# Decayed cumulative sum of a matrix product: the last five lumps of output on other queues

## The chip, the cores and the metric

The kernel runs on one core of one Trainium2 chip. The metric is the time of one execution in microseconds (us), the median of several runs; less is better. The core has a matrix engine (TensorE, PE in the profile), a vector engine (VectorE, DVE), an activation engine (ScalarE, ACT), a general engine (GpSimd, POOL) and an engine that here only issues transfers (SyncE, SP). Each engine carries out its own instructions in order. A transfer (DMA) is an instruction in the order of the engine that issues it; the data are then moved by 16 DMA engines that all queues share.

## The reference

```python
B, S, D = (16, 2048, 1024)
xw = x @ w
out[:, 0, :] = xw[:, 0, :]
for t in range(1, S):
    out[:, t, :] = decay[None, :] * out[:, t - 1, :] + xw[:, t, :]
```

All arrays are float32. `decay` holds 1024 values between 0.05 and 0.95. The output is 134 MB.

## The kernel before, in words

Time is cut into chunks of 512 steps, 64 in all (4 for each of the 16 batches), and most of the work takes two chunks of a batch together. The 1024 output columns are cut into 8 groups of 128. A **tile** is one group of columns for one pair of chunks: 128 partitions (columns) by 1024 steps. The last two chunks are taken singly, so the last 16 tiles have 512 steps. There are 31 x 8 + 16 = 264 tiles, and the text counts the last ones from the end: tile -1 is the last, tile -16 the first of the short ones.

For each tile TensorE multiplies eight blocks of w with x (converted to bf16 and transposed beforehand) into PSUM (`matmul`, L131). Then the recurrence runs along time, in one of two ways. An unpaired tile is scanned by VectorE straight from PSUM (`run`, L221). A paired tile has the scan over every second step only: ScalarE copies PSUM out (`copy`, L183, letter `p`) and multiplies the even steps by the decay (`odd`, `g`, through `decayed`, L169), GpSimd adds (`join`, L196, `j`), VectorE scans with the squared decay (`scan`, L201, `S`), and ScalarE (`even`, `h`) and GpSimd (`fill`, L246, `c`) compute the steps between. `z` sets the first value, `k` saves the last one for the next chunk. At last VectorE turns the tile back so that time lies on partitions (`back`, L258, `B`), writing it into an output buffer `ot`.

Four tiles, that is 512 columns, share one output buffer, which is written out as a whole: this is a **lump**, with the class `Outlet` to hold it. There are four such buffers, taken in turn, so a lump's first transpose must wait until the lump four before it has been stored. A lump of long tiles is 2 MB, a lump of short ones 1 MB. It is stored by four DMAs, one for each quarter of the partitions (`q`, 32 partitions each), in runs of 512 bytes. They are issued when the fourth tile has been transposed, in `store` (L282). Nearly all lumps are stored by SyncE alone, in the order of quarters 0, 2, 1, 3. Four lumps near the end (tiles -24 to -9) alternate between SyncE (quarters 0 and 1) and GpSimd (quarters 2 and 3); the next one (tiles -8 to -5) goes by SyncE alone in eight DMAs, each with half of the steps. The four last tiles are not transposed by VectorE: the function `ending` (L387 to L393) has TensorE transpose them, ScalarE and VectorE copy them out by turns, and SyncE store them in four DMAs of 256 KB.

The order of the work of ScalarE, VectorE, GpSimd and SyncE around each tile is written out by hand in the table `agenda`: a row for each step, with the deeds in their order, a letter and a tile. Everything issued is kept in that order on its engine (`pin`), and the semaphores between engines, among them the counters on which DMAs report that they are done, are set by the framework when it schedules the program. DMAs of SyncE and ScalarE use eight such counters, taken in turn; GpSimd's DMAs use eight others. A DMA waits until the DMA that had its counter before it has landed.

The rows of `agenda` for the last steps, before the change, with the transposes (`B`) of the lumps in question:

```python
-19: "p-20 g-20",
-18: "j-20 S-19 S-20 k-19 B-19",
-13: "p-14 S-16 g-14 j-14 S-15 h-16 k-16 c-16",
-9: "p-10 k-12 g-10 h-12 B-11 j-10 k-11",
-6: "p-7 g-7 j-7 B-10 B-8",
-3: "p-4 B-6 g-4 B-5 j-4",
-1: "S-2 h-4 c-4 a-1 b-1 V",
```

Of the kernel before, what the change touches and what calls it, by code (L numbers as in the profile page):

```python
# [14 lines left out]
def _ap(ap_obj: bass.AP, new_ap, extra_offset=0):  # L15
    return dataclasses.replace(
        ap_obj,
        ap=[list(p) for p in new_ap],
        offset=ap_obj.offset + extra_offset,
    )  # L20
# [5 lines left out]
def kernel(  # L26
# [26 lines left out]
    nc = tc.nc  # L53
    pin = tc.keep_in_program_order
    B, S, D = x.shape
# [3 lines left out]
    P = 32  # L59
# [6 lines left out]
    R = K // 2  # L66
    CH = D // 2
    CR = CH // NQ
# [7 lines left out]
    def ring(pool, name, count, shape, dtype=FP32):  # L76
        i = turns[name] = turns.get(name, -1) + 1
        return pool.tile(shape, dtype, name=f"{name}{i % count}")

    def quad(q):  # L80
        return slice(q * P, (q + 1) * P)
# [12 lines left out]
    def ot_tile(nj):  # L94
        return ring(sb, "ot", 4, [128, nj, CR])
# [29 lines left out]
    def matmul(ps, n, k, xt, t0=0, t1=TL, start=0, pairs=None):  # L125
        if pairs is None:
            rhs = xt[:, k // 2, k % 2, t0:t1]
        else:
            rhs = pairs[:, k // 2, t0 // P:t1 // P, :, k % 2].rearrange("p j i -> p (j i)")
        lhs = wsb[:, k, n].rearrange("p q i -> p (q i)")  # L130
        pin(nc.tensor.matmul(  # L131
            out=ps[:, t0:t1] if ps.shape[1] >= t1 else ps,
            lhsT=lhs,
            rhs=rhs,
            start=(k == 0 and t0 == start),
            stop=(k == K - 1),
        ))
# [3 lines left out]
    class Tile:  # L141
# [3 lines left out]
        def __init__(self, g, n, ps, outlets):  # L145
            self.b, self.t0 = chunks[g[0]]
            self.T = TL * len(g)
            self.n, self.ps, self.outlets = n, ps, outlets
            self.paired = n % R != R - 1
            if len(tiles) in flips or len(tiles) - len(slots) in flips:  # L150
                self.paired = not self.paired
            self.turn = len(tiles)
            self.lot = sum(t.paired for t in tiles)
            self.prev = None if self.t0 == 0 else last[n]
            if self.t0 + self.T < S:
                last[n] = const.tile([128, 1], FP32, name=f"keep{n}", bufs=2)
                self.keep = last[n]
            else:
                self.keep = None
# [106 lines left out]
    class Outlet:  # L266


        def __init__(self, ns, nj, half=0, queues=(nc.sync,), pieces=1):
            self.pieces = pieces  # L270
            self.ns, self.missing, self.half = ns, set(ns), half
            self.nj, self.t0, self.queues = nj, half * nj * P, queues
            self.ot = ot_tile(nj)

        def store(self, b, t0):
            n0 = self.ns[0]
            c0 = n0 % R * P
            size = len(self.ns) * P
            nj = self.nj // self.pieces
            for j in range(0, self.nj, nj):  # L280
                for i, q in enumerate((0, 2, 1, 3)):
                    pin(self.queues[i % len(self.queues)].dma_start(  # L282
                        out=_ap(out, [[D, P], [P * D, nj], [1, size]],
                                (b * S + t0 + self.t0 + j * P) * D
                                + n0 // R * CH + q * CR + c0),
                        in_=self.ot[quad(q), j:j + nj, c0:c0 + size]))

# [1 line left out]
    size = M * CH  # L291
# [37 lines left out]
    for q in range(NQ):  # L329
        pin(nc.sync.dma_start(  # L330
            out=rows[q * P:q * P + R],
            in_=_ap(decay, [[P, R], [CH, 2], [1, P]], q * CR)))
# [71 lines left out]
    slots = [(g, n) for g in groups[:-1] for n in range(K)]  # L404
    slots += [([c], n) for c in groups[-1] for n in range(K)]
    tiles = []

    def turn_and_load(c):
# [24 lines left out]
        "d": square_again,  # L433
        "I": identity,
        "V": ending,
        "p": lambda s: tiles[s % len(slots)].copy(),
        "g": lambda s: tiles[s % len(slots)].odd(),
        "z": lambda s: tiles[s % len(slots)].zero(),
# [42 lines left out]
        32: "c29 S31 S30 h30 B29 c30 p32 g32 z32 j32 B30 B31 L L",  # L481
        33: "p33 g33 z33 j33 S32 h32 c32 k32 L L",
        -20: "z-20",
        -19: "p-20 g-20",
        -18: "j-20 S-19 S-20 k-19 B-19",
        -17: "h-20 k-20 c-20 S-18 k-18",
        -16: "I S-17 B-20 p-16 g-16 j-16",
        -15: "z-15 k-17 B-18 z-16",
        -14: "p-15 g-15 z-14 j-15 B-17",
        -13: "p-14 S-16 g-14 j-14 S-15 h-16 k-16 c-16",  # L490
        -12: "S-13 h-15 k-15 c-15 S-14 k-13",
        -11: "p-12 B-13 h-14 B-15 g-12 c-14 k-14 B-16",
        -10: "j-12 B-14 z-12 S-12 z-10 S-11",
        -9: "p-10 k-12 g-10 h-12 B-11 j-10 k-11",
        -8: "S-9 c-12 S-10 k-9",
        -7: "z-7 B-12 h-10 k-10 B-9 c-10 S-8",
        -6: "p-7 g-7 j-7 B-10 B-8",
        -5: "S-7 S-6 h-7 c-7",
        -4: "z-4 S-5 B-7",
        -3: "p-4 B-6 g-4 B-5 j-4",  # L500
        -2: "S-3 S-4",
        -1: "S-2 h-4 c-4 a-1 b-1 V",
    }
# [24 lines left out]
    def rest(s):  # L528
        do = [f"S{s - 1}"] if tiles[s - 1].paired else []
        do.append(f"C{s - 1}")  # L530
        if tiles[s - 2].paired:
            do.append(f"B{s - 2}")
        return do + [f"B{s - 1}"] + later.get(s, []) + ["L"] * len(loads)
# [7 lines left out]
    for step, (g, n) in enumerate(slots):  # L541
        T = TL * len(g)
        left = step - len(slots)
        if n % R == 0:
            ns, nj = range(n, n + R), T // P
            both = -6 * R <= left < -2 * R
            outlets = [Outlet(ns, nj, queues=(nc.sync, nc.gpsimd) if both else (nc.sync,),
                              pieces=2 if left == -2 * R else 1)]
        if left == -R:
            outlets = []  # L550
        if step == 0:
            heads = [ring(psp, "ps", 3, [128, T]) for _ in range(3)]
            firsts = [ps[:, 0:TL] for ps in heads] + [spares[0]]
            seconds = [ps[:, TL:T] for ps in heads] + [spares[1]]
            for j0, j1 in halves:
                for k in range(0, K, 2):
                    for i in range(R):
                        matmul(firsts[i], i, k, xt_of[0], j0 * P, j1 * P, pairs=xw_of[0])
            for k in range(1, K, 2):
                for i in range(R):  # L560
                    matmul(firsts[i], i, k, xt_of[0])
            for k0 in range(0, K, 2):
                for i in range(R):
                    for k in (k0, k0 + 1):
                        matmul(seconds[i], i, k, xt_of[1], 0, H * P,
                               pairs=xw_of[1] if k0 < 4 else None)
            for i in range(R):
                for k in range(K):
                    matmul(seconds[i], i, k, xt_of[1], H * P, TL, H * P,
                           pairs=xw_of[1] if i < 2 else None)  # L570
        if step < R:
            ps = heads[n] if n < 3 else tuple(spares)
        else:
            if step == K + 1:
                ps = nexts
            elif len(g) == 2 or n % R < 3:
                ps = ring(psp, "ps", 3, [128, T])
            else:
                ps = ring(psp, "spare", 1, [128, TL])
            todo = [(k, l) for k in range(K) for l in range(len(g))]  # L580
            if step < K:
                todo.sort(key=lambda kl: kl[0] % 2)
            elif step == K:
                todo = []
                nexts = ring(psp, "ps", 3, [128, T])
                for l in range(len(g)):
                    for i, both in enumerate((ps, nexts)):
                        for k in range(K):
                            matmul(both[:, l * TL:(l + 1) * TL], n + i, k, xt_of.get(g[l]),
                                   pairs=xw_of[g[l]] if g[l] in (3,) else None)  # L590
            elif step == K + 1:
                todo = []
            if left == -1:
                ps = tuple(both[:, t:t + TL // 2] for t, both in zip(
                    (0, TL // 2), (ps, ring(psp, "ps", 3, [128, TL]))))
                for t, half in zip((0, TL // 2), ps):
                    for k in range(K):
                        matmul(half, n, k, xt_of[g[0]], t, t + TL // 2, t)
                todo = []
            for k, l in todo:  # L600
                matmul(ps[:, l * TL:(l + 1) * TL], n, k, xt_of[g[l]])
        tiles.append(Tile(g, n, ps, outlets))
        do = agenda.get(step, agenda.get(left) if left >= -20 else None)
        if do is None:
            do = usual(step)
        else:
            do = do.split()
            if left == -20:
                do = rest(step) + do
        perform(do)  # L610
# [29 lines left out]
```

## Time and profile before

| | us |
|---|---|
| median of 3 runs | 908.35 (907.34 to 908.75) |
| span of the profiled execution | 907.2 |
| PE busy | 892.8 (98%) |
| DVE busy | 826.3 (91%) |
| ACT busy | 686.2 (76%) |
| POOL busy | 663.0 (73%) |
| POOL, issues of output stores (L282), 8 of them | 5.7 busy, 5.5 idle before them |
| DMA, mean over the span | 226 GB/s |

No time is recorded for the profiled execution itself beside its span; the span is 1.2 us below the median of the runs. The span is that of the instructions on the core's engines, the waits for the last transfers among them. "Busy" is the time in which an engine has an instruction under way; issues of DMAs by SyncE and ScalarE are not counted. A line of the profile gives the source line, the engine, the operation, what it writes and reads, its count, the busy time and the mean of one, and then the idle time before it with the work whose end ended most of it. SPq and ACTq are the queues in which SyncE and ScalarE issue transfers; an issue is over when its descriptors are handed on, and "to landing" is the time from the start of the issue until the data are reported stored.

### The profile page before, as it was taken

The page shows a single profiled execution, that of the slowest core. Times are in us where ns is not written, and L with a number is a line of the kernel's source. Part 1 is how long each engine was busy: PE and PEld are TensorE (multiplying, and loading weights), DVE is VectorE, ACT ScalarE, POOL GpSimd, SP SyncE. Part 2 cuts the span into 40 slices and gives each one's busy share as a digit, 9 for nine tenths or more (in the row PEclk, how much of TensorE's full clock was granted, in tenths as well). Part 3 has the DMA queues.
Part 4 walks back from the last instruction along what each step waited for, and adds up shares of the span by engine and source line. Part 5 has one row for each costly group of instructions (what it writes and reads, how often), then busy time and mean ns, then how long its engine had stood idle before and what let it go on. Part 6 is the DMA issues. An engine that isn't in the chain of part 4 may idle for free.

```text
span 907.2 us, 12004 instructions
## 1 busy us (share of the span) xinstructions
PE 892.8 (98%) x4119; PEld 411.4 (45%) x4201; DVE 826.3 (91%) x628; ACT 686.2 (76%) x955; POOL 663.0 (73%) x763
## 2 busy tenths in 40 slices
PE   9999999999999999999999999999999999999996
PEld 5444444444444444444444444444444444444443
DVE  4999989999999999899999999999999999999996
ACT  4889867777777877877877778778778778777742
POOL 7888678877777767768677777777677686776562
PEclk9999999999999999999999999999999999999999
DMA  9999999999999999999999999999999999999788
GB/s 194 194 215 220 227 215 220 215 238 255 249 250 254 241 243 259 247 244 228 227 233 227 227 232 227 226 232 233 220 230 231 228 231 223 232 229 207 153 161 211
DMA packets 397230, 204.77 MB, mean 226 GB/s; under 512 B 8816, under 2 KB 395376, under 8 KB 397168
## 3 DMA queue, kind: packets, MB, share of 16 engines
q1 hardware_dynamic: 258960, 131.62, 59.6%
q0 software_dynamic: 137920, 71.85, 58.1%
q8 instruction: 33, 0.54, 0.2%
q10 hardware_dynamic: 288, 0.52, 0.2%
q14 instruction: 29, 0.24, 0.1%
HBM read 138.42 MB, written 134.22 MB: 301 GB/s over the span
## 4 chain that ended last, share of the span: by engine, by line
PE 93%; DMA 2%; POOL 1%; issue 1%; DVE 1%; ACT 0%; POOLq 0%; DVEq 0%
PE ps L131 93%; DMA xb<-in_x_dram 2%; POOL ot L299 1%; POOL xb L105 1%; PE spare L131 1%; DVE xw L115 0%; ACT xt L123 0%; ACT xs L183 0%; DVE so L201 0%; PE spare L387 0%; DVE ot L258 0%; ACT h L169 0%; PE ps L387 0%; POOLq L635 0%; POOL xs L196 0%
## 5 line engine op out<-in xcount | busy, mean ns | idle before, releaser
L131 PE MATMUL ps<-xt,wsb 128*128 128x512 bf16 x3942 | 863.5, 378 | 4.7 <-ACT h L169 0.2
L131 PEld LDWEIGHTS <-wsb 128*128 128x128 bf16 x4152 | 405.9, 98 | 479.9 <-ACT wsb L306 0.8
L196 POOL TENSOR_TENSOR xs<-h,xs 128x512 f32<-128x512 f32 (+1 forms) x190 | 243.0, 1279 | 181.8 <-ACT h L169 79.4
L183 ACT COPY xs<-ps 128x1024 f32<-128x1024 f32 (+1 forms) x190 | 189.4, 997 | 155.3 <-PE ps L131 144.2
L258 DVE STREAM_TRANSPOSE ot<-so 128x1024 f32<-128x1024 f32 (+1 forms) x260 | 300.1, 1191 | 2.1 <-POOL so L190 1.1
L246 POOL TENSOR_TENSOR so<-h,xs 128x512 f32<-128x512 f32 (+1 forms) x190 | 241.4, 1272 | 39.0 <-ACT h L169 25.7
L123 ACT COPY xt<-xw 128x2048 bf16<-128x2048 bf16 (+1 forms) x136 | 242.3, 1790 | 7.8 <-DVE xw L115 7.6
L105 POOL DMA_DIRECT2D xb<-in_x_dram x264 | 174.3, 661 | 3.3 <-DMA ot<-in_w_dram 1.1
L169 ACT ACTIVATE h<-so,dec 128x512 f32<-128x512 f32 (+1 forms) x190 | 145.4, 766 | 27.7 <-DVE so L201 24.4
L115 DVE STREAM_TRANSPOSE xw<-xb 128x2048 f32<-128x2048 f32 (+1 forms) x78 | 147.4, 1901 | 5.5 <-DMA xb<-in_x_dram 5.5
L201 DVE TENSOR_TENSOR_SCAN so<-spare,keep,xs 128x512 f32<-128x512 f32 (+1 forms) x97 | 120.0, 1239 | 27.7 <-POOL xs L196 27.4
L201 DVE TENSOR_TENSOR_SCAN so<-spare,xs 128x512 f32<-128x512 f32 x93 | 113.3, 1220 | 27.6 <-POOL xs L196 24.6
L169 ACT ACTIVATE h<-ps,dec 128x512 f32<-128x512 f32 (+1 forms) x190 | 130.3, 686 | 0.0
L221 DVE TENSOR_TENSOR_SCAN so<-dec,ps 128x1024 f32<-128x1024 f32 x34 | 76.8, 2261 | 1.0 <-ACT h L169 1.0
L221 DVE TENSOR_TENSOR_SCAN so<-dec,keep,ps 128x1024 f32<-128x1024 f32 (+1 forms) x35 | 75.9, 2169 | 0.1
L250 ACT COPY keep<-so 128x1 f32<-128x1 f32 x136 | 25.3, 189 | 9.9 <-DVE so L221 9.4
L192 ACT COPY so<-keep 128x1 f32<-128x1 f32 x97 | 18.4, 191 | 2.6 <-DVE ot L258 2.4
L131 PE MATMUL ps<-xw,wsb 128*128 128x256 bf16 (+1 forms) x68 | 11.2, 301 | 0.1
L190 POOL MEMSET so<- 128x1 f32 x93 | 10.7, 117 | 0.6 <-DVE ot L258 0.6
L131 PE MATMUL spare<-xt,wsb 128*128 128x512 bf16 (+1 forms) x48 | 10.0, 335 | 0.0
L282 POOL DMA_DIRECT2D out_dram<-ot x8 | 5.7, 722 | 5.5 <-DVE ot L258 5.1
L299 POOL DMA_DIRECT2D ot<-in_w_dram x12 | 6.6, 546 | 3.3 <-DMA xb<-in_x_dram 2.0
(38 smaller groups left out, 44.5 us busy)
## 6 DMA issues: line engine op xcount, KB each, us to landing
out_dram<-ot SPq DMA_DIRECT2D x244, 512.0 KB, 10.9
xb<-in_x_dram POOLq DMA_DIRECT2D x248, 256.0 KB, 7.8
xb<-in_x_dram POOLq DMA_DIRECT2D x16, 128.0 KB, 5.8
out_dram<-ot POOLq DMA_DIRECT2D x4, 512.0 KB, 11.6
ot<-in_w_dram POOLq DMA_DIRECT2D x12, 128.0 KB, 5.1
out_dram<-ot SPq DMA_DIRECT2D x4, 256.0 KB
out_dram<-ot POOLq DMA_DIRECT2D x4, 256.0 KB, 8.5
out_dram<-ot SPq DMA_DIRECT2D x8, 128.0 KB, 4.3
```

The costliest lines, as they stand in the source:

```text
L105: pin(nc.gpsimd.dma_start(out=xb_of[c][quad(q), j0:j1], in_=_ap(x, [[D, P], [P * D, j1 - j0], [1, CQ]], (b * S + t0 + j0 * P) * D + q * CQ)))
L115: pin(nc.vector.transpose(out=dst.rearrange("p (m j i) -> p j m i", m=M, i=P)[:, j0:j1, m0:m1], in_=src.rearrange("p (j m c) -> p j m c", ...
L123: pin(copy(out=xt_of[c][:, m0:m1, :, j0 * P:j1 * P], in_=src))
L131: pin(nc.tensor.matmul(out=ps[:, t0:t1] if ps.shape[1] >= t1 else ps, lhsT=lhs, rhs=rhs, start=(k == 0 and t0 == start), stop=(k == K - 1),))
L169: pin(nc.scalar.activation(out=h, in_=src, func=mybir.ActivationFunctionType.Copy, scale=dec[:, self.n:self.n + 1]))
L183: pin(nc.scalar.copy(out=self.xs, in_=self.ps))
L196: pin(nc.gpsimd.tensor_tensor(out=odds, in0=self.g, in1=odds, op=ALU.add))
L201: pin(nc.vector.tensor_tensor_scan(out=so[:, 3:T + 2:2], data0=squares[-1][:, n:n + 1].to_broadcast([128, T // 2]), data1=self.xs[:, 1:T:2 ...
L221: pin(nc.vector.tensor_tensor_scan(out=so[:, t + 2:t + 2 + size], data0=dec[:, n:n + 1].to_broadcast([128, size]), data1=ps, initial=befor ...
L246: pin(nc.gpsimd.tensor_tensor(out=self.so[:, 2:T + 2:2], in0=self.h, in1=self.xs[:, 0:T:2], op=ALU.add))
L250: pin(nc.scalar.copy(out=self.keep, in_=self.so[:, self.T + 1:self.T + 2]))
L258: pin(nc.vector.transpose(out=outlet.ot[:, :, c0:c0 + P], in_=self.so[:, 2 + t0:2 + t0 + nj * P].rearrange("p (i t) -> p i t", t=P)))
```

## The change

The four lumps that went half by SyncE and half by GpSimd, and the fifth that went by SyncE in eight pieces, now all go half by SyncE (quarters 0 and 1, issued as before when the lump is complete) and half by ScalarE (quarters 2 and 3). ScalarE's half has a deed of its own, `O`, with a place of its own in the table: `O-21` stands for the lump whose last tile is -21. `O-21` comes after `g-20`, `O-17` after `g-14`, `O-13` before `p-10`, `O-9` after `g-7` and `O-5` after `g-4`. The pieces are gone. Nothing else in the table is moved.

```diff
-        def __init__(self, ns, nj, half=0, queues=(nc.sync,), pieces=1):
-            self.pieces = pieces
+        def __init__(self, ns, nj, half=0, shared=False):
             self.ns, self.missing, self.half = ns, set(ns), half
-            self.nj, self.t0, self.queues = nj, half * nj * P, queues
+            self.nj, self.t0, self.shared = nj, half * nj * P, shared
             self.ot = ot_tile(nj)
 
         def store(self, b, t0):
+            self.b, self.at = b, t0 + self.t0
+            self.send(nc.sync, (0, 1) if self.shared else (0, 2, 1, 3))
+
+        def send(self, queue, quads):
             n0 = self.ns[0]
             c0 = n0 % R * P
             size = len(self.ns) * P
-            nj = self.nj // self.pieces
-            for j in range(0, self.nj, nj):
-                for i, q in enumerate((0, 2, 1, 3)):
-                    pin(self.queues[i % len(self.queues)].dma_start(
-                        out=_ap(out, [[D, P], [P * D, nj], [1, size]],
-                                (b * S + t0 + self.t0 + j * P) * D
-                                + n0 // R * CH + q * CR + c0),
-                        in_=self.ot[quad(q), j:j + nj, c0:c0 + size]))
+            for q in quads:
+                pin(queue.dma_start(
+                    out=_ap(out, [[D, P], [P * D, self.nj], [1, size]],
+                            (self.b * S + self.at) * D + n0 // R * CH + q * CR + c0),
+                    in_=self.ot[quad(q), :, c0:c0 + size]))
...
+        "O": lambda s: tiles[s % len(slots)].outlets[0].send(nc.scalar, (2, 3)),
...
-        -19: "p-20 g-20",
+        -19: "p-20 g-20 O-21",
...
-        -13: "p-14 S-16 g-14 j-14 S-15 h-16 k-16 c-16",
+        -13: "p-14 S-16 g-14 O-17 j-14 S-15 h-16 k-16 c-16",
...
-        -9: "p-10 k-12 g-10 h-12 B-11 j-10 k-11",
+        -9: "O-13 p-10 k-12 g-10 h-12 B-11 j-10 k-11",
...
-        -6: "p-7 g-7 j-7 B-10 B-8",
+        -6: "p-7 g-7 j-7 B-10 O-9 B-8",
...
-        -3: "p-4 B-6 g-4 B-5 j-4",
+        -3: "p-4 B-6 g-4 B-5 j-4 O-5",
...
-            both = -6 * R <= left < -2 * R
-            outlets = [Outlet(ns, nj, queues=(nc.sync, nc.gpsimd) if both else (nc.sync,),
-                              pieces=2 if left == -2 * R else 1)]
+            outlets = [Outlet(ns, nj, shared=left >= -6 * R)]
```

On each engine the rest of the instructions keeps its order. GpSimd loses its eight stores, ScalarE gains ten, and SyncE has two stores instead of eight for lump -5.

## The prediction

> Six lumps of output matter, named by their last tile counted from the end of the 264: -25 (2 MB, by SyncE alone in both kernels), -21 and -17 (2 MB), -13, -9 and -5 (1 MB). Times are us from the start of the profiled span.
>
> **What bounds the kernel now.** First the page's parts 2 and 4:
>
> ```profile
> PE   9999999999999999999999999999999999999996
> PE 93%; DMA 2%; POOL 1%; issue 1%; DVE 1%; ACT 0%; POOLq 0%; DVEq 0%
> ```
>
> TensorE sets the pace until the last tiles; a change to stores can only act in the tail. The chain's last piece there is `DVE h L391`, the last copy of the ending, which ends at 899.73; the span ends at 907.16. VectorE and SyncE's queue in the tail (start, length, engine, line, operation, count):
>
> ```profile
> 882.86 0.71 DVE L258 STREAM_TRANSPOSE ot<-so 128x512 f32<-128x512 f32 x1
> ...
> 887.66 1.27 DVE L258 STREAM_TRANSPOSE ot<-so 128x512 f32<-128x512 f32 x2
> ...
> 899.04 0.69 DVE L391 COPY h<-spare 128x512 f32<-128x512 f32 x1 [0.18 <-PE spare L387]
> ```
>
> ```profile
> 893.73 6.97 SPq L282 DMA_DIRECT2D out_dram<-ot  x8
> 900.80 1.45 SPq L393 DMA_DIRECT2D out_dram<-xb  x3
> 902.66 0.33 SPq L393 DMA_DIRECT2D out_dram<-h  x1
> ```
>
> Two things are to be seen. From 877.7 to 896.6 VectorE has no bracketed wait: a stall there moves the ending by as much. And SyncE is late: the eight stores of lump -5 occupy it until 900.70, so the last store is issued 2.93 after its copy is ready. From that issue to the end it is 4.50.
>
> How fast a half lump leaves, from narrow windows of the DMA issues (KB each, us from issue to landing). The first two are lump -21's two stores by SyncE, the last two the first two of the lump before -25:
>
> ```profile
> out_dram<-ot SPq DMA_DIRECT2D x1, 512.0 KB, 4.8
> out_dram<-ot SPq DMA_DIRECT2D x1, 512.0 KB, 7.5
> ...
> out_dram<-ot SPq DMA_DIRECT2D x1, 512.0 KB, 4.5
> out_dram<-ot SPq DMA_DIRECT2D x1, 512.0 KB, 6.8
> ```
>
> The issues of such a pair lie 0.36 apart, so a following 512 KB takes 3.06 where one queue sends partitions 0-63 alone (7.5 - 4.8 + 0.36) and about 2.6 where the halves alternate.
>
> Last, waits of SyncE's queue in the first 40 us:
>
> ```profile
> SPq L282 <- DMA ot<-in_w_dram: 1.9, 1, 1.9
> ```
>
> The very first output store waited for a load of w. It needs no data of it; they share a completion counter, and that load was issued by ScalarE. So the counters are shared by the two queues.
>
> **The change, part by part.** *GpSimd's eight issues go*: 5.7 us of POOL in all (part 5 of the page, L282). VectorE waits for POOL there once, 0.22 at 877.66: a gain of at most 0.2, lost again below. Their packets no longer start some 6 us after the issue.
>
> *Lump -5 by two stores of SyncE instead of eight*: 6.97 falls to 0.32 + 0.57 (the two issues at 861.66), or to 0.32 + 1.91 if the queue is full (the two at 880.96). By itself this lets the last store go at 899.8, 2.9 earlier.
>
> *Ten issues on ScalarE*: no issue of this shape by ScalarE is in the trace. Its two loads of w took 0.42 and 0.45; the same stores on SyncE take 0.89 a pair to 2.23 a pair. Bounds 0.9 and 2.2 for each pair; I take 0.9, the empty-queue row, because ScalarE's queue is new and mostly empty. Behind them: for -21, k-19, 3.17 idle ahead of it, so nothing; for -17, h-16 (875.72), 0.5 late, hidden because GpSimd, which adds after it, no longer issues 1.6 us of stores; for -13, p-10 (881.19), whose result VectorE needs at 884.66, 1.5 in hand (uncovered: up to 0.7 on VectorE); for -9, h-7 (889.60), up to 0.9 late, and its transpose comes only at 891.83; for -5, h-4 (895.54), free at 0.9, 0.4 late at 2.2.
>
> *The waits that come with it decide.* The built program lists what every DMA waits for. The eight counters of SyncE's and ScalarE's DMAs go round in the order in which the scheduler lists them, and each DMA waits until its counter's previous user has landed. Before, that user was eight stores of SyncE back and always done. In the changed program ScalarE's stores are listed far ahead of where they run, between SyncE's of earlier lumps, so SyncE, which issues in order, waits for stores that ScalarE issues later:
>
> - -25's first store waits for the second ScalarE store of -21; -25's third for the first of -17
> - -21's first for the second of -17
> - -13's and -9's second ones for ScalarE stores of -9, and -5's second for the first of -5; the ending's second for the second of -5
>
> Before, -25 left from 848.08 on. Now, step by step:
>
> 1. ScalarE is free for -21 at 861.77 (its h ends 861.08 + 0.69); its second store is issued at 862.13 and lands 7.5 later: 869.6.
> 2. So -25's first two stores go at 869.65, 21.6 late; the third still waits.
> 3. For -17 ScalarE is free at 875.25: first store lands 4.8 later, 880.05, second (issued 875.6, +7.4 by that lump's own row) 883.05.
> 4. -25's third goes at 880.1, the fourth at 880.45. Alone the fourth lands 6.8 later, 887.25. Half of lump -13 (0.52 MB, ScalarE) leaves beside it; at the 242 GB/s of 892 to 896 that is up to 2.1 more, 889.4. I take the middle, 888.3.
> 5. Lump -25 lies in the same one of four output buffers as lump -9, so the transpose at 882.86, -9's first, must wait for 888.3: **5.4 us of stall on VectorE** (4.4 to 6.5). GpSimd, ScalarE and TensorE have room behind it: TensorE's next tile into PSUM is held some 2.5, and VectorE reads it later than that.
> 6. -5's first transpose (888.25, second of the x2) needs the buffer of -21, whose SyncE half follows -25's fourth store in the queue: 888.3 + 2 x 3.06 = 894.4, against 888.25 + 5.4 = 893.7. Stall 0.7; together 6.1.
> 7. The last copy ends at 899.73 + 6.1 = 905.8. SyncE's second store of -5 waits for ScalarE's first, issued at 893.70 + 6.1 = 899.8 and landed by 904.6 at 4.8. Then four issues of 0.47 end no sooner than the last copy allows: last issue about 906.0, against 902.66, which is +3.3, span 910.5.
> 8. The same queue as a sum: after -25's third lands (884.9), SyncE still has eight times 0.52 MB (one of -25, two each of -21 and -17, one each of -13, -9, -5): 20.8 at 2.6, 24.5 at 3.06, so 905.7 to 909.4; the ending's 1 MB takes 2.8 more at the 375 GB/s that its packets show from 902 to 904, and 1.15 follow the last landing as now: span 909.7 to 913.3, middle 911.5.
>
> The later of 7 and 8 decides: 911.5, less some overlap of the two queues, say 911.2. Sum: 907.16 + 4.0. The median of the runs lies 1.2 above this span, so 908.35 + 4.0 = **912.3**.
>
> The Trainium skill, "DMA: Bandwidth & Descriptors", section "Issuing engines are not separate DMA queues", holds that stores from several engines share the same DMA engines and that spreading them saves only time to issue. By it the sum would have no speed-up from a second queue and stand at the upper end of step 8, 914.5; the rows of lump -21 show 171 GB/s from one queue (0.52 MB in 3.06) and, where GpSimd's joins at 888 to 892, 224, so they go against it in part.
>
> **Rivals.** *As the change is meant* (faster): the counters hold nobody up. For it: the stores of before never waited for one. Against: the list of waits, and the first store of the kernel. SyncE would be free at 896, the last store go at 899.8: 908.35 - 2.9 = 905.5.
>
> *The hold costs little* (same): SyncE is held, but DMA engines left idle from 856 on catch up; -25's fourth store lands at 886.6, the stall is 3.7, and the overlap of two queues hides the rest of step 8. Last issue 903.5, 0.9 later than now: 909.2. For it: DMA share 0.36 at 860 to 864, so there is room. Against: 2 MB more stand behind 880 than before.
>
> *ScalarE stalls too* (slower still): while one queue's issue is blocked, the other's is as well. The trace has issues of 2.1 and 1.9 on SyncE when its queue is full (835.24, 881.32), and SyncE is full from 883 on. ScalarE's pair of -9 then takes up to 3 us more, h-7 and lump -5's transposes slip by 2 and the pair of -5 delays h-4 by another 2: 912.3 + 4 = 916.3. Against it: at 0.74 both queues issued at once, 0.42 and 0.39, no longer than one alone. The Trainium skill, "Perfetto Trace Analysis", section "DMA Instruction — HWDGE (DVE, Sync)", says that one descriptor generator is shared by two sequencers and locked while in use; by it this case would hold whenever SyncE blocks. The two equal issues at 0.74 do not show the lock.
>
> **Numbers.** Forecast 0.64, own range 909.5 to 915.5; as meant 0.10; hold costs little 0.14; ScalarE stalls too 0.12. No change that this measurement can tell is within 0.2%, 906.5 to 910.2. Faster is the first rival: 0.10. Same is the cheap hold and the forecast's low edge: 0.15. Slower 0.75. Range: 908.5, below which lies mainly the first rival, to 917.
>
> **What would show it.** SyncE silent from about 840 to 869, with -25's first stores at 869 to 870 and third at 880; a VectorE wait of 4 to 7 before the L258 transpose that stood at 882.86, released by a DMA out of ot; the last L393 issue near 906; ScalarE's issues near 0.3 and 0.6. Wrong: SyncE's store at 848.08 still there, or that wait under 3; or ScalarE's issues of 2 and more.

## The result and the profile after

| | before | after |
|---|---|---|
| median of 4 runs each, on one chip | 908.55 (907.34 to 908.90) | 918.90 (918.83 to 919.12) |
| ratio, 95% interval | | 1.0116 (1.0103 to 1.0129) |
| span of the profiled execution | 907.2 | 917.1 (time of this execution 918.92) |
| last copy of the ending ends | 899.73 | 906.97 |
| last store of the ending issued | 902.66 | 913.01 |

The kernel is 10.4 us slower. All times in the text are us from the start of the profiled span; events ahead of the trouble lie some 0.5 earlier after than before (ScalarE is free for lump -21 at 861.22 instead of 861.77).

The page of the kernel after, its span, parts 2 (TensorE and the DMA rate in 40 slices of 22.9 us) and 4 (the chain):

```profile
span 917.1 us, 12001 instructions
...
PE   9999999999999999999999999999999999999984
...
GB/s 194 196 215 216 232 234 218 216 250 242 245 250 247 249 246 246 255 241 222 226 230 228 232 224 230 226 228 233 225 231 229 228 225 232 234 220 174 60 195 205
...
PE 93%; DMA 3%; issue 1%; POOL 0%; ACTq 0%; ACT 0%; SPq 0%; DVE 0%; POOLq 0%; DVEq 0%
```

Up to the last four slices it is the kernel before. Slice 38 (848 to 871) moves 60 GB/s, and the next two are full: output that left at 848 now leaves at the end. A view of the DMAs from 848 to 871 in 40 slices shows the gap itself:

```profile
GB/s 0 0 0 0 0 0 0 0 0 0 0 0 0 0 0 0 0 0 0 0 0 0 0 0 84 174 177 172 177 186 173 183 173 176 162 30 0 95 161 176
...
out_dram<-ot ACTq DMA_DIRECT2D x2, 512.0 KB, 7.0
out_dram<-ot SPq DMA_DIRECT2D x2, 512.0 KB, 5.5
```

For 14 us nothing moves. Then ScalarE's half of -21 leaves at some 175 GB/s, and only after it has landed do SyncE's first two stores of -25 go. The waits of SyncE's queue from 840 to 917 (us in total, times, the longest), and its stores on the timeline (start, length, count; the third line is from a later window and begins inside the second):

```profile
SPq L283 <- DMA out_dram<-ot: 43.7, 4, 29.1
```

```profile
868.67 2.17 SPq L283 DMA_DIRECT2D out_dram<-ot  x2
...
893.78 10.93 SPq L283 DMA_DIRECT2D out_dram<-ot  x3
...
902.41 7.01 SPq L283 DMA_DIRECT2D out_dram<-ot  x5
...
909.53 3.39 SPq L393 DMA_DIRECT2D out_dram<-xb  x3
913.01 0.55 SPq L393 DMA_DIRECT2D out_dram<-h  x1
```

Before, SyncE waited for no output store from 840 on. Here it waits 43.7 for them: -25's first store goes at 868.67 (of the 29.1 ahead of it, some 8 would have been a wait for data, since -25 left at 848.08 before). The middle group holds a second standstill: its first issue ends at 896.64, the next one, -13's second store, starts at 902.41, when ScalarE's first store of -9 (issued at 895.25) has landed. Five stores of lumps and the ending's four go behind it. VectorE and ScalarE (in brackets the idle time before, and what ended it):

```profile
889.74 0.71 DVE L258 STREAM_TRANSPOSE ot<-so 128x512 f32<-128x512 f32 x1 [7.92 <-DMA out_dram<-ot]
...
894.53 1.52 DVE L258 STREAM_TRANSPOSE ot<-so 128x512 f32<-128x512 f32 x2
...
906.28 0.69 DVE L391 COPY h<-spare 128x512 f32<-128x512 f32 x1 [0.18 <-PE spare L387]
```

```profile
861.22 0.95 ACTq L283 DMA_DIRECT2D out_dram<-ot  x2
...
880.31 2.05 ACTq L283 DMA_DIRECT2D out_dram<-ot  x2
...
895.25 2.37 ACTq L283 DMA_DIRECT2D out_dram<-ot  x2
...
900.97 1.75 ACTq L283 DMA_DIRECT2D out_dram<-ot  x2
```

So the 10.4 us are two things. VectorE stands still for 7.92 at the first transpose of -9, and the last copy ends 7.24 later. And the last store is issued 6.04 behind that copy instead of 2.93, which is 3.11 more. Together 10.35 (the spans of the two profiled executions differ by 9.99, since the way from the last issue to the end is 0.36 shorter). The experiments below are read by these two, the **end of the last copy** and the **lag** of the last issue behind it:

| kernel | median | last copy ends | last issue | lag |
|---|---|---|---|---|
| before | 908.55 | 899.73 | 902.66 | 2.93 |
| after | 918.90 | 906.97 | 913.01 | 6.04 |
| e1_listed | 906.15 | 899.72 | 900.44 | 0.72 |
| e6_stall | 912.70 | 907.32 | 907.46 | 0.14 |
| e14_late_wait | 913.80 | 905.65 | 907.11 | 1.46 |
| e10_quarters | 915.41 | 907.41 | 909.12 | 1.71 |
| e11_late_gpsimd | 920.00 | 910.87 | 912.51 | 1.64 |
| e9_sync_alone | 905.62 | 899.80 | 900.29 | 0.49 |
| e12_order | 908.87 | 899.32 | 902.96 | 3.64 |

### The profile page after: what moved, and what is told of

Same layout as the page of the kernel before. It is cut to its first block, busy times and chain, and to the rows that moved or that the text cites. A ratio compares the mean times of both kernels' runs of the same rounds, so it can differ in the third digit from the quotient of the medians.

```text
span 917.1 us, 12001 instructions
## 1 busy us (share of the span) xinstructions
PE 893.8 (97%) x4119; PEld 411.4 (45%) x4201; DVE 825.5 (90%) x628; ACT 685.5 (75%) x955; POOL 656.5 (72%) x755
## 4 chain that ended last, share of the span: by engine, by line
PE 93%; DMA 3%; issue 1%; POOL 0%; ACTq 0%; ACT 0%; SPq 0%; DVE 0%; POOLq 0%; DVEq 0%
PE ps L131 93%; DMA out_dram<-ot 2%; DMA xb<-in_x_dram 1%; DMA ot<-in_w_dram 1%; PE spare L131 0%; ACTq L283 0%; PE spare L387 0%; SPq L283 0%; POOL ot L299 0%; ACT h L169 0%; PE ps L387 0%; POOLq L634 0%; POOL xs L196 0%; POOL xb L105 0%; DVE h L391 0%
## 5 line engine op out<-in xcount | busy, mean ns | idle before, releaser
L324 PE MATMUL spare<-idle 128*128 128x512 bf16 x22 | 7.0, 492 | 1.2 <-DVE idle L314 1.2
```

## The experiments

Ratios are to runs of the kernel before on the same chip (medians there 908.8 to 909.1), with 95% intervals.

**e1_listed: the counters in the order of issue.** The instructions and their order on each engine stay those of the changed kernel. An edge that only the scheduler sees, with no semaphore, lists each output store behind the one before it in the program.

```diff
+    listed = []
+    def listed_after(dma):
+        if listed:
+            tc.add_manual_dep(
+                dma.ins, listed[-1].ins.name,
+                mybir.DependencyInfo(mybir.DependencyClass.NoSync,
+                                     mybir.DependencyReason.DATA),
+                reason="one round of counters")
+        listed.append(dma)
...
-                pin(queue.dma_start(
+                dma = pin(queue.dma_start(
...
+                listed_after(dma)
```

> The changed kernel with one more edge for the scheduler: each output store is listed behind the one before it, so the completion counters go round in the order in which the stores run. No engine's order changes. Theory (counters): SyncE's store of lump -25 is back near 848, the VectorE wait of 7.9 us is gone, the last L393 issue comes within 0.5 us of the last copy, and the time is 905.0 to 907.0, below the 908.5 of the kernel before. Rival (ScalarE's issues, or two queues slowing each other): the wait on VectorE shrinks, but ScalarE's pairs stay at 2 us and the time stays above 912.

Measured 906.15 (905.94 to 906.73), ratio 0.9972 (0.9961 to 0.9982): 12.8 below the changed kernel, and faster than the kernel before. The waits of SyncE's queue from 840 on, and its first stores and ScalarE's:

```profile
SPq L294 <- DVE ot L258: 42.9, 6, 12.3
SPq L405 <- ACT xb L403: 3.9, 2, 3.7
```

```profile
848.20 5.80 SPq L294 DMA_DIRECT2D out_dram<-ot  x4
```

```profile
861.79 1.08 ACTq L294 DMA_DIRECT2D out_dram<-ot  x2
```

No wait for an output store is left: SyncE waits for VectorE's transposes and ScalarE's copies, that is for data. Lump -25 leaves at 848.20 as before. All of the loss, then, hangs on which DMA shares a counter with which, and none on ScalarE's ten issues by themselves.

**e2_small and e2_small_listed: the counters without the move of data.** The lumps go by SyncE and GpSimd as before; ScalarE sends only 16 KB of each of quarters 2 and 3, at the places of the change, GpSimd the rest. Lump -5 goes in the same way. The second kernel adds the edges of e1 for SyncE's and ScalarE's stores.

```diff
+            if self.shared:
+                self.send(nc.sync, (0, 1), 0, self.nj)
+                self.send(nc.gpsimd, (2, 3), 1, self.nj)
+            else:
+                self.send(nc.sync, (0, 2, 1, 3), 0, self.nj)
```

> The kernel before, still with GpSimd's half, except that ScalarE sends one thirty-second of the two quarters (32 of 1024 or 512 steps, 16 KB a store) at the places O, and SyncE sends lump -5 in two stores. The counters are listed out of order again: the third and fourth stores of lump -29 wait for ScalarE's of -21, the third and fourth of -25 for those of -17. Theory (counters): SyncE is held as in the changed kernel although ScalarE moves almost nothing: -29's third store moves from 835 to about 864, the transpose that stood at 882.86 waits 2 to 6 us for lump -25, time 911 to 918. Rival (ScalarE's halves themselves cost it): within 2 us of the kernel before, 906.5 to 910.5.

> The same as the run with small ScalarE stores, but listed in the order in which they run. Theory (counters): no hold, 905.5 to 908.5 (lump -5 has two stores by SyncE, GpSimd carries the rest). Rival (ScalarE's issues at these places cost time whatever they carry): as slow as the unlisted one.

Measured 920.93, ratio 1.0133 (1.0119 to 1.0147), and listed in order 908.89, ratio 0.9999 (0.9990 to 1.0008). The first lies above what either theory gave it, the second 0.4 above its theory's range. In the first, GpSimd, which issues here, also does sums of the recurrence, and the last copy ends at 911.22. The pair tells it plainly: 12.0 us between two kernels whose engines do the same things in the same order, while a store of ScalarE carries 16 KB, 1/32 of a quarter of a 2 MB lump.

**e5_one_piece: lump -5 alone.** The kernel before with `pieces=1`, so that SyncE stores -5 in four DMAs instead of eight.

```diff
-                              pieces=2 if left == -2 * R else 1)]
+                              pieces=1)]
```

> The kernel before with lump -5 in four stores of 256 KB by SyncE instead of eight of 128 KB, nothing else. By the prediction's own term, SyncE's 6.97 us of issues for this lump hold the end: four stores take about 0.3 + 3 x 1.5 = 4.8, so the last L393 issue comes about 2 us earlier and the time is 906 to 907. Rival (the transfers and not the issues hold the end): the issues get longer as the queue is full, and the time stays within 0.5 us of before.

Measured 907.77, ratio 0.9986 (0.9977 to 0.9995), between the two expectations. Its four issues take 0.32, 1.72, 1.62 and 1.84, 5.5 instead of 6.97, and the last issue of the ending goes 0.98 earlier, at 901.68. The pieces are worth about 1 us of the 2.93 that the kernel before loses behind its last copy.

**e6_stall: the stall alone.** e1_listed, and VectorE transposes the last chunk of x three times more into its finished buffer, ahead of `B-11`.

```diff
-        -9: "O-13 p-10 k-12 g-10 h-12 B-11 j-10 k-11",
+        -9: "O-13 p-10 k-12 g-10 h-12 T63 T63 T63 B-11 j-10 k-11",
```

> The listed kernel (no hold) with three more turns of the last chunk of x on VectorE, 2.3 us each, ahead of lump -9's first transpose: 6.9 us of extra VectorE time at the place of the wait, and nothing else. Theory (two holds add up): the ending's copies come 6.5 to 7 later and the time is 912.3 to 913.5, so the VectorE wait alone makes about 7 of the changed kernel's 12.8 us over the listed one. Rival (TensorE or GpSimd take up part of it): below 911.

```profile
882.45 6.98 DVE L115 STREAM_TRANSPOSE xw<-xb 128x2048 f32<-128x2048 f32 x3
```

Measured 912.70, ratio 1.0041 (1.0027 to 1.0054). 6.98 of VectorE at this place cost 6.6 us, nearly one for one, and the last copy ends even later than in the changed kernel (it waits 1.02 for TensorE, whose granted clock is 0.52 from 904 to 908; in the changed kernel it waits 0.18 at 1.00). But the lag is 0.14: with no waits behind it, SyncE's queue is empty when the copies are done. So the stall makes 6.6 of the 12.8 between e1 and the changed kernel; 6.2 are to be found in the queue.

**e4_late_listed and e8_late_free: one hold taken away at a time.** In the first, ScalarE's stores of -13, -9 and -5 are listed in order and those of -21 and -17 are not; in the second only those of -9 and -5 are. (The expectation of e4 counts those of -17 among the listed ones too; the kernel that ran left them free.)

```diff
+                if queue is nc.sync or self.last in (-13, -9, -5):   # e4
+                if queue is nc.sync or self.last in (-9, -5):        # e8
+                    listed_after(dma)
```

> The changed kernel with ScalarE's stores of -17, -13, -9 and -5 listed behind their own lump's half, and only those of -21 left free. SyncE still waits at -25's first store for ScalarE's second of -21 (about 868.6), but then all four of -25 may go; -21's and -17's SyncE halves wait for ScalarE's of -17, the later ones for nobody. Theory (what costs is that lump -25's buffer is not free for the transpose at 882): the four stores land by 880, the VectorE wait of 7.9 falls below 1.5 although 2 MB still leave 20 us late, and the time is 906.5 to 910. Rival (the late bytes cost by themselves, whoever waits): 914 or more.

> The changed kernel with only ScalarE's stores of -9 and -5 listed behind their own lump's half: the waits of -25 and -21 are exactly those of the changed kernel, and the late waits, -13's second store for ScalarE's first of -9 and those behind it, are gone. Theory (two holds add up): VectorE still waits 7.5 to 8.5 us at lump -9's first transpose, but SyncE does not stand still from 896.6 to 902.4, the last L393 issue comes 3 to 5 us earlier than 913, and the time is 913.5 to 916.5. Rival (the transfers fill the tail, SyncE's wait only hides it): SyncE's issues become longer by as much, 918 to 919.

Measured 918.25, ratio 1.0101 (1.0088 to 1.0115), and 918.11, ratio 1.0103 (1.0087 to 1.0118). Both theories miss, and both times lie in the ranges of the rivals, by which the data left for the end cost the time, whoever waits. But the way is another one: in both, the last issue comes 0.13 behind the last copy, and it is the copies that are late. The edges did not take a hold away, they gave it to the other engine. In e4 (waits from 840 on, then ScalarE's stores):

```profile
DVE ot L258 <- DMA out_dram<-ot: 5.2, 1, 5.2
...
DVE ot L258 <- POOL so L246: 5.1, 2, 4.2
```

```profile
881.66 3.15 ACTq L295 DMA_DIRECT2D out_dram<-ot  x2
898.94 3.35 ACTq L295 DMA_DIRECT2D out_dram<-ot  x2
902.34 0.53 ACT L169 ACTIVATE h<-so,dec 128x256 f32<-128x256 f32 x1 [13.27 <-DMA out_dram<-ot]
```

ScalarE's own stores now carry the counters of SyncE's late ones. The multiply that stands behind the pair of -9 begins at 902.34, after a DMA has landed; GpSimd is late after it, and VectorE waits 5.1 for GpSimd besides 5.2 for a buffer. In e8, VectorE waits 7.99, SyncE has no standstill, and ScalarE's stores of -5 wait in its order, at 903.97 and on: the multiply for the last tile that stands behind them begins at 906.37, and the last copy ends at 911.93. With copies so late, neither time says what SyncE's late standstill costs. The landings of e8 say something: without a standstill SyncE's last store of a lump is issued by 906.44 instead of 909.43, but it lands at 912.72 instead of 913.67, only 1.0 sooner. Of the three orders tried, only the one in which the stores run helps.

**e10_quarters: both halves in each queue.** The changed kernel, with its waits, but SyncE sends quarters 0 and 2, ScalarE 1 and 3.

```diff
-            self.send(nc.sync, (0, 1) if self.shared else (0, 2, 1, 3))
+            self.send(nc.sync, (0, 2) if self.shared else (0, 2, 1, 3))
...
-        "O": lambda s: tiles[s % len(slots)].outlets[0].send(nc.scalar, (2, 3)),
+        "O": lambda s: tiles[s % len(slots)].outlets[0].send(nc.scalar, (1, 3)),
```

> The changed kernel, with SyncE's queue sending quarters 0 and 2 of each of the last five lumps and ScalarE's quarters 1 and 3, so that each queue reaches both halves of the partitions. Waits on counters as in the changed kernel. Theory (a queue that holds one half of the partitions alone is slow, and this sized the tail): SyncE's issues after 888 take nearer 1.0 to 1.2 us for 256 KB than the 1.5 to 1.9 of the changed kernel, the stall of VectorE stays at 5 to 8 us, the tail is shorter, 912 to 916.5. Rival (the waits on counters size it, whichever partitions a queue holds): 917 to 920.5.

Measured 915.41, ratio 1.0072 (1.0057 to 1.0087), in the theory's range and 3.5 below the changed kernel. SyncE's queue still waits 44.7 for output stores, VectorE 7.2 at the same transpose, and the last copy ends 0.44 later than in the changed kernel; it is the lag that falls, from 6.04 to 1.71. The windows from 892 to 896 (in each, the busy time and count of five engines, the granted clock, the DMA engines' busy share, GB/s), in which SyncE's queue is almost alone, of the changed kernel and of this one:

```profile
892.00:896.00 4.00, 3.40 (x11) 1.20 (x10) 3.88 (x7) 1.47 (x4) 1.47 (x2) 0.61 0.94 188
```

```profile
892.00:896.00 4.00, 3.95 (x14) 1.64 (x14) 4.00 (x6) 1.40 (x4) 1.48 (x2) 0.76 0.94 226
```

The same busy share, 188 and 226 GB/s. The standstill is there in both, from 896.64 to 902.41 and from 894.68 to 900.24. It ends 2.2 sooner, the five stores after it are issued in 6.1 instead of 7.0, the ending's four in 3.3 instead of 4.0: of the 3.9 by which the last issue is earlier, 2.2 are the earlier end of the wait. The expectation for the single issue was off, though: after 888 those that stand behind a full queue take 1.2 to 3.1. That the copies end 0.44 later after a shorter stall is TensorE's part: its granted clock is 0.52 from 904 to 908, and the last copy waits 1.02 for it.

**e11_late_gpsimd: no late standstill.** The changed kernel, with the second halves of -9 and -5 issued by GpSimd, whose DMAs have counters of their own.

```diff
+            if self.last >= -9:
+                self.send(nc.gpsimd, (2, 3))
...
-        -6: "p-7 g-7 j-7 B-10 O-9 B-8",
+        -6: "p-7 g-7 j-7 B-10 B-8",
...
-        -3: "p-4 B-6 g-4 B-5 j-4 O-5",
+        -3: "p-4 B-6 g-4 B-5 j-4",
```

> The changed kernel, with the second halves of lumps -9 and -5 issued by GpSimd, whose DMAs count on counters of their own, and without the two late places in ScalarE's order. The waits before lump -13 stay as they are, those of SyncE's late stores are for ScalarE's stores of -13, which land before. Theory (5.8 us of SyncE standing still and the late issues of ScalarE are what the end adds to the stall): VectorE still waits 7 to 8.5 us for lump -25's buffer, SyncE doesn't stand still after 893, its last issue of the ending is within 3.5 us of the last copy, 912 to 915.5. Rival (the data left over at the end sets it, by whichever queue): 917 to 920.

```profile
DVE ot L258 <- DMA out_dram<-ot: 8.2, 2, 7.9
...
POOL out_dram L286 <- DVE ot L258: 4.0, 2, 3.0
...
PE spare L390 <- POOL so L246: 3.6, 1, 3.6
```

Measured 920.00, ratio 1.0121 (1.0106 to 1.0137): the theory misses in time, and the time is at the upper end of the rival's range. Of the theory's parts, VectorE's wait of 7.9, SyncE at work throughout after 893 and the short lag (1.64) came; but GpSimd waits for the transposes before it can issue, its sums are late, TensorE waits 3.6 for them and the last copy ends 3.9 later than in the changed kernel. Its place in GpSimd's order has its own price, and with copies so late the lag says little of the queue. SyncE's stores of lumps tell more: the last is issued by 907.42 instead of 909.42. So without the standstill 2.0 are gained in the queue, and its single issues, of one half of the partitions still, take 1.6 to 2.6 after 895.

**e14_late_wait: the late wait on an empty queue.** e6_stall, and in it a real wait: SyncE's second store of -13 until ScalarE's first of -9 has landed, with SyncE's stores of -9 behind it.

```diff
+    def late():
+        lumps[-9].send(nc.scalar, (2, 3))
+        first = listed[-2]
+        lumps[-13].send(nc.sync, (1,))
+        tc.add_manual_dep(
+            listed[-1].ins, first.ins.name,
+            mybir.DependencyInfo(mybir.DependencyClass.Sync,
+                                 mybir.DependencyReason.DATA),
+            reason="wait")
+        lumps[-9].send(nc.sync, (0, 1))
...
-        -6: "p-7 g-7 j-7 B-10 O-9 B-8",
+        -6: "p-7 g-7 j-7 B-10 Q-9 B-8",
```

> The kernel with the chained listing and the added stall of VectorE (912.7), and in it the late wait of the changed kernel alone: SyncE's second store of lump -13 waits until ScalarE's first store of -9 has landed, and SyncE's stores of -9 go behind it. Theory (the late standing still has a price of its own behind the stall): SyncE stands still from some 881.5 to 902, five stores of 256 KB and the ending's four are behind it, at 1.2 to 1.6 us each its last issue of the ending is at 910.5 to 912.5 instead of 907.5, 915.5 to 918.5. Rival (what follows the stall has room, the backlog of the early waits and the queue with one half alone set the rest): 912 to 914.5.

```profile
SPq L309 <- DVE ot L258: 32.8, 5, 12.2
SPq L309 <- DMA out_dram<-ot: 16.7, 2, 13.0
```

Measured 913.80, ratio 1.0055 (1.0038 to 1.0072), the rival. SyncE waits 16.7 for stores and the time rises by 1.1 over e6, which ran on another chip; the two intervals overlap. In the profiled executions the lag is 1.32 longer than in e6, and the copies end 1.67 earlier, in part because the granted clock is 1.00 from 904 to 908 and not 0.52 as in e6. The store waited for was issued at 894.29 and landed at 897.2, 2.9 later, with little else moving (0 GB/s from 888 to 892); in the changed kernel it took 7.1, in e10 5.3. Five stores of lumps stand behind the wait here as there. What is missing is the data that the DMA engines still had to move.

**e9_sync_alone and e12_order: one queue, and the order of the quarters.** All output by SyncE in four stores a lump, no `O`, nothing by GpSimd. In e9 the quarters go 0, 2, 1, 3; in e12 those of the last five lumps go 0, 1, 2, 3.

```diff
-            outlets = [Outlet(ns, nj, shared=left >= -6 * R)]
+            outlets = [Outlet(ns, nj, shared=False)]
```

```diff
-            self.send(nc.sync, (0, 1) if self.shared else (0, 2, 1, 3))
+            self.send(nc.sync, (0, 1, 2, 3) if self.last >= -21 else (0, 2, 1, 3))
```

> All lumps by SyncE alone, four stores each (lump -5 too), no store by ScalarE or GpSimd in the tail. If a second queue saves only time to issue and none in the transfers, the stores of the tail leave as fast as in the listed kernel, and only SyncE's longer issues are added: 906 to 907.5. If one queue alone moves these runs of 512 bytes more slowly (2.5 to 3.06 us for 512 KB), the 5.2 MB from 875 on take about 25 us, and the ending's stores wait: 908 to 911.

> All output by SyncE's queue alone, as in the run before it of that kind (905.62), but the last five lumps in the order of quarters 0, 1, 2, 3 instead of 0, 2, 1, 3, so that two stores to the same half of the partitions follow each other. No wait on another queue's DMA anywhere. Theory (it is the alternation of halves that lets one queue move 245 to 252 GB/s): the last lumps take longer, their four issues some 5.5 to 7 us for 1 MB instead of 4.2, 907.5 to 912. Rival (a queue takes the halves side by side whatever their order, since several stores are in flight): 905 to 906.5.

Measured: e9 905.62 (905.44 to 906.07), ratio 0.9964 (0.9952 to 0.9977); e12 908.87, ratio 1.0001 (0.9991 to 1.0010). Two windows of e9, then the same of e12:

```profile
884.00:888.00 4.00, 4.00 (x21) 1.76 (x18) 4.00 (x6) 1.86 (x6) 1.13 (x3) 1.00 0.96 254
888.00:892.00 4.00, 3.95 (x19) 1.84 (x19) 4.00 (x6) 0.74 (x3) 1.20 (x2) 1.00 0.98 245
```

```profile
884.00:888.00 4.00, 4.00 (x21) 1.82 (x19) 4.00 (x7) 1.86 (x6) 1.48 (x2) 1.00 0.88 201
888.00:892.00 4.00, 3.95 (x19) 1.80 (x19) 4.00 (x6) 1.24 (x4) 0.74 (x1) 1.00 0.95 229
```

With the order of the quarters alone, 254 and 245 GB/s become 201 and 229, the last lump's four issues take 4.8 instead of 3.3, and the lag grows from 0.49 to 3.64, which is the 3.2 us. e9 is the fastest version here, with no second queue at all, though its interval overlaps with that of e1: whether two queues in good order are worth less than one, or the same, stays open. Either beats both kernels.

## Why the prediction was right in direction and short in size

The hold, the stall and the sign were the forecast's; the time is 6.6 over the predicted 912.3 and 1.9 over the end of the range. The step that failed is step 8, the sum of what was left to store: it left out ScalarE's share.

**Steps 1 to 3** held within about 1: ScalarE's second store of -21 issued at 861.59 (862.13 was predicted) and landed at 868.6 (869.6), -25's first stores at 868.67 (869.65), -17's landings at some 879 and 881.9 (880.05 and 883.05).

**Steps 4 and 5**, the stall, were short by 2.5: 7.92 for 5.4. The third store of -25 went at 878.85, 1.25 sooner than predicted, but the buffer came free at 889.7 and not at 888.3. I had let its last stores and the half lump beside them leave at 242 GB/s; the windows 884 to 888 and 888 to 892 show 197 and 212. The other 1.0 is that VectorE was at the place at 881.8 and not at 882.9.

**Step 6**, 0.7 more for -21's buffer, was hardly there: the two transposes at 894.53 take 1.52 together instead of 1.27. So the copies end 7.24 later where 6.1 was said. e6 confirms the exchange rate: 6.98 on VectorE is 6.6 of time.

**Step 8 failed, the queue's part.** Step 7 let the lag behind the last copy shrink from 2.93 to 0.2, and step 8, which decided, had SyncE's last store of a lump landed between 905.7 and 909.4. It landed at 913.67, and the lag grew to 6.04. The step counted the eight halves that SyncE's queue still had at 884.9 and took ScalarE's stores at nothing; 0.3 was even taken off for the overlap of the queues. Two windows of the changed kernel, from 884.9 to that landing and SyncE's standstill alone (columns as in e10's windows), and the queues in the first of them (packets, MB, share; q1 is SyncE's, q10 ScalarE's):

```profile
884.90:913.67 28.77, 14.86 (x76) 7.71 (x75) 16.80 (x21) 4.91 (x13) 3.79 (x6) 0.88 0.95 207
896.64:902.41 5.77, 5.77 (x36) 3.21 (x33) 5.75 (x8) 1.46 (x4) 1.47 (x2) 1.00 0.93 228
```

```profile
q1 hardware_dynamic: 8437, 4.59, 73.9%
q10 hardware_dynamic: 2705, 1.34, 20.8%
```

The DMA engines were busy nearly all the time (share 0.95), at 207 GB/s. That is 2.5 for each 0.52 MB, so the step's 2.6 to 3.06 was not too fast. The amount was too small: ScalarE's 1.34 MB are 2.6 more halves through the same engines. With them the step gives, as an estimate, 27.5 to 32.4 instead of 20.8 to 24.5, a landing between 912.4 and 917.3.

The part on the waits had also named the second store of -13 waiting for ScalarE's of -9, and no step put a price on it. SyncE stands still for 5.8 with five stores behind, but the DMA engines go on with what is queued, at a share of 0.93: little transfer time is lost there, which fits e8 (the landing 1.0 sooner without the standstill) and e14 (1.1 for a wait with nothing queued). What else sizes the end is the rate: with both halves in each queue (e10) 6.05 MB leave from 884.9 to the landing at 909.98, 241 GB/s, and the lag is 1.71.

Set against e1, the 12.8 us are: 6.6 the stall (e6), 3.5 that each queue holds one half of the partitions (e10), 1.1 the late wait on an empty queue (e14, with the reservations made there). 1.6 are not assigned; the parts aren't independent, so the sum needn't close.

**The costs at nothing.** ScalarE's pairs took 0.95, 0.94, 2.05, 2.37 and 1.75 where 0.9 was taken from the empty queue and 2.2 was the other bound. For the first two lumps the choice was right, for the last three the full-queue row was the near one. e1 shows the same ten issues with the stores in order: no cost in sum.

**Lump -5 by fewer stores** was put at 2.9 earlier for the last issue; four stores instead of eight gave 0.98 (e5). Issues of 256 KB behind a full queue take 1.6 to 1.8, so there is less to save than the empty-queue pair suggests; two stores alone weren't tried.

**The rivals.** *As meant* has its conditions met in e1, which came to 906.15 where 905.5 was given: the reason against it, the list of waits, was the whole reason. *The hold costs little* fell with the stall. *ScalarE stalls too* came nearest in time, which is luck: the copies are not late by ScalarE (their delay is below the stall). In the changed kernel ScalarE's first store of -13 took 0.32 at 880.31, while an issue of SyncE was under way from 879.21 to 881.02, and in e1 an issue of SyncE at 861.78 and one of ScalarE at 861.79 took 0.32 and 0.38, so that two queues issue side by side. The lock of which the Trainium skill speaks ("Perfetto Trace Analysis", section "DMA Instruction — HWDGE (DVE, Sync)") isn't seen in these two pairs. Its other rule, "DMA: Bandwidth & Descriptors", section "Issuing engines are not separate DMA queues", agrees with e9 in time: one queue 905.62, two 906.15. In the rate the runs differ from it: from 864 to 868 and from 880 to 884 e1's two queues moved 280 and 285 GB/s, e9's one 190 and 212. I had set the rule aside because one queue showed 171 GB/s and two 224, and read that as the worth of a queue; part of that worth lay in the halves, as e9's 254 from one queue shows.

## What to carry to other kernels

Before a DMA is given to another engine's queue, list for every DMA which one had its completion counter before: if the framework deals counters in its own order, a store that is listed early makes an earlier store of another queue wait for a later one, and that cost 12.8 us here with the data and the engines' orders unchanged. List transfers in the order in which they will run, then read the waits again, since taking away some of these waits moved them to the next engine (e4, e8). When you add up what a queue still has to move, add what the other queues move beside it. Where stores pile up in one queue, let it cover all partitions in turn (e10, e12); in e1, where two queues ran side by side, one half for each cost nothing that the time shows.

## What the runs showed of the hardware

- One queue carries more when stores to partitions 0-63 and 64-127 alternate: 245 to 254 GB/s against 201 to 229 in two halves one after the other (e9, e12, 884 to 892; from 864 to 872 it is 190 and 240 against 177 and 194), and some 175 to 190 for one half alone (848 to 871 and 892 to 896 in the changed kernel). The DMA engines are as busy in the slow case (share 0.94 at 188 GB/s, 0.94 at 226 in e10). What makes the packets of one half longer wasn't tried.
- The granted clock dipped to 0.61 from 892 to 896 in the changed kernel, right behind 4.05 us in which TensorE waited for VectorE, and was 1.00 again from 900; in e9 it stays at 1.00 from 876 to 900. The last copy there is late by about VectorE's delay, so no time is assigned to the clock. In e6 and e10 it was 0.52 from 904 to 908, and seven transposes of the ending on TensorE took 1.55 and 1.57 instead of 0.93 in the changed kernel.
